# Head-pair attention with a merged window, the residual kept in the output tensor, and sums of FFN2 weights made by DMA

## The chip, the cores and the metric

The kernel runs on one NeuronCore of a Trainium2 chip. The core has five engines with queues of their own: TensorE (PE; its weight loads are shown as PEld), VectorE (DVE), ScalarE (ACT), GpSimd (POOL) and SyncE (SP). SP does no arithmetic here; it issues DMAs, and POOL and ACT issue some too. Each engine works through its instructions in order and waits at semaphores. Arithmetic works on SBUF (128 partitions), PE writes to PSUM, of which each bank holds 128 x 512 float32, and DMAs move data between device memory and SBUF, or within memory. The metric is the device time of one execution in microseconds (us).

## The reference

One decoder layer on 1024 tokens of width 1024, with 16 learned meta tokens put in front (1040 rows in all) and dropped from the output. All in float32:

```python
u = rmsnorm(h, g_pre_mix)
z = u @ w_in                                   # [q 512 | k 128 | v 128 | x 512 | y 512]
attn = sliding_window_attention_with_sinks(q, k, v, sinks)   # 8 heads of 64, 2 KV heads, window 128
rec = gelu(yr) * rg_lru(causal_conv4(xr), ...)               # 512 channels
h = h + rmsnorm(concat(attn, rec) @ w_out, g_post_mix)
u = rmsnorm(h, g_pre_ffn)
f = square(relu(u @ w_ff1)) @ w_ff2            # 1024 -> 4096 -> 1024
out = (h + rmsnorm(f, g_post_ffn))[16:]
```

Attention works in blocks of 128 queries. A query sees the 128 keys up to and with itself, so keys of its own block and of the one before: of each pair of key columns that stand at the same place in the two blocks, exactly one is in the window. The softmax's denominator has one more term, a sink per head. Query heads 0 to 3 use KV head 0, heads 4 to 7 KV head 1.

## The kernel before

**Precision.** A float32 matmul is made of three passes over operands that are split in a high and a low part (`split`, lines 93 to 100: ACT copies with rounding, L95, and DVE subtracts, L98; `mm3`, lines 122 to 128, the passes L124, L125 and L126).

**Order.** The program is written as straight code over tiles in pools; a scheduler makes the order of each engine's queue from it: among the instructions that are ready, it takes the one that stands first in the program, and a DMA into a buffer is ready when the buffer is free. `deferred(1000)` makes some work stand later than written, `behind(name, ins)` pins an order by hand. A tag of the pool `slab` (`raw`, `ws`, `a`, `b`, `c`, `d`, `e`) is a set of buffers that rotate.

**Stages.** (1) Norm, transpose and the projections of K, V, the first pair of Q and the first channels of x, in four pieces of the tokens (`project`, lines 220 to 231). (2) Attention in 4 x 2 rounds (`scores` and `attend`, lines 503 to 594), with the remaining projections as filling for PE (`next_fill`). (3) Gates and recurrence of the LRU. (4) W_out, the norm, and the residual h, which `out_norm` (lines 801 to 823) writes to `h_dram` (L818). (5) FFN1 as seven products of blocks in place of eight (a Strassen scheme: sums of weight blocks and of activation blocks): a first pass with `prep_a`, whose combined weights go to `s_dram` and come back in the second pass (`for p in range(16)`, lines 1066 to 1082, `fetch_b` three tiles ahead), and a third over `third`. (6) FFN2 as seven products too (`PLAN`, lines 1101 to 1110), each in 8 steps over q; a step of `PLAN` names one block of W2 or a sum or difference of two. `fetch_2` (lines 1112 to 1126) loads the terms three steps ahead over SP, or adds the second term by an accumulating DMA from POOL (L1121) for some q; else `prep_2` adds on DVE (L860 through `combine`).

**A round of attention** handles query heads j and j + 4, one of each KV head, and four blocks. Q of a head has its high part on 64 partitions and its low part on the other 64; K's high part is on both halves, its low part on one, with zeros on the other (`put_k`, lines 352 to 357). `scores` makes per head and block a 128 x 256 score tile (own block and the one before), adds the mask and takes the maximum on DVE (L538), the exponential and its sum on ACT (L82), and scales by the reciprocal on DVE (L551). `attend` transposes 128 x 128 pieces on PE (L566), two per block and head, splits them, multiplies with V (`av`, L577), and adds V's high and low results (L591, L592). A round's `attend` stands after the next round's `scores`.

**The end.** Output rows of the second half (four blocks of 128) are finished during FFN2 by `finish_early` (lines 1186 to 1195): scale, a DMA from POOL that adds `h_dram`'s rows in SBUF (L1194), and a store from SP (L1195). Rows of the first half end with the last product: `finish_half` (lines 1199 to 1212) loads h and squares one half of the columns, `finish_late` (lines 1214 to 1244) adds the last product, takes the root on POOL (L169, L1234), multiplies by the gain (POOL, L1237, for three of four), and scales and adds h on DVE (L1241) before two stores. In the last three steps PE goes through row block after row block (lines 1308 to 1312).

Of the kernel before, what the change touches and what calls it, by code (L numbers as in the profile page):

```python
# [9 lines left out]
F32 = mybir.dt.float32  # L10
# [27 lines left out]
def hybrid_layer(  # L38
# [212 lines left out]
    for h in range(2):  # L251
        nc.gpsimd.memset(f32(kl[h][HALF[1 - h]]), 0.0)

    zero = slot("ws", [P, 512])
    nc.vector.memset(zero, 0.0)
    km = const.tile([P, 4, P], F32R, name="km")
    vm = const.tile([P, 2, P], F32R, name="vm")
    nc.vector.tensor_copy(km.rearrange("p a b -> p (a b)"), zero)
    nc.vector.tensor_copy(vm.rearrange("p a b -> p (a b)"), zero[:, :256])
# [65 lines left out]
    rq = fetch([(Q_COL, HD), (Q_COL + 4 * HD, HD)], "e")  # L325
# [26 lines left out]
    def put_k(hh, lo, src):  # L352
        for h in range(2):
            r, o = HALF[h], HALF[1 - h]
            nc.scalar.copy(hh[h][r], src[r])
            nc.vector.tensor_copy(hh[h][o], src[r])
            nc.vector.tensor_tensor(lo[h][r], src[r], f32(hh[h][r]), op=ALU.subtract)  # L357

    def sink_k(acc, t0, n):
        o = 0  # L360
        if t0 == 0:
            m = slice(0, NMETA)
            put_k(
                [km[:, 0, m], km[:, 1, m]], [km[:, 2, m], km[:, 3, m]], acc[:, m]
            )
            o = NMETA
# [4 lines left out]

    def sink_v(acc, t0, n):
        nc.scalar.copy(vt[:, t0 : t0 + n], acc)
# [25 lines left out]
    for b in range(4):  # L399
# [23 lines left out]
        done.append(last_mm[0])  # L423

# [3 lines left out]
    for c in range(NLRU):  # L428
# [18 lines left out]
    nc.gpsimd.memset(mask1[:, 0:P], NEG)  # L447
    nc.gpsimd.memset(mask1[:, 0:NMETA], 0.0)
    nc.gpsimd.affine_select(
        out=mask1[:, 0:NMETA], in_=mask1[:, 0:NMETA], pattern=[[1, NMETA]],  # L450
        compare_op=ALU.is_gt, fill=NEG, base=P - NMETA, channel_multiplier=-1,
    )
    nc.gpsimd.tensor_copy(mask1[:, P:256], mask[:, P:256])
# [32 lines left out]
    nc.tensor.transpose(pv[:NMETA, :P], vt[:, :NMETA], ident)  # L486
    put_v([vm[:NMETA, 0, :], vm[:NMETA, 1, :]], pv[:NMETA, :P])
# [15 lines left out]
    def scores(j, half, q):  # L503
        sn = [slot("c", [P, 4, 257]) for _ in range(2)]
        negm = small.tile([P, 2, 4], F32, name="negm", tag="negm")
        den = small.tile([P, 2, 4], F32, name="den", tag="den")
        rden = small.tile([P, 2, 4], F32, name="rden", tag="rden")
        for h in range(2):
            nc.vector.tensor_copy(
                sn[h][:, :, 256], nsink[:, j + 4 * h : j + 4 * h + 1].to_broadcast([P, 4])  # L510
            )
        for bp in range(2):
            for h in range(2):
# [13 lines left out]
                for i in range(2):  # L527
                    b = 4 * half + 2 * bp + i
                    if b == 0:
                        qk(sp_[:, i, 0:P], b, km[:, h, :], km[:, 2 + h, :])  # L530
                        qk(sp_[:, i, P:256], b, khh[h][:, 0:P], kl[h][:, 0:P])
                    else:
                        c = slice((b - 1) * P, (b + 1) * P)
                        qk(sp_[:, i, :], b, khh[h][:, c], kl[h][:, c])
                for i in range(2):
                    b = 4 * half + 2 * bp + i
                    k = 2 * bp + i
                    nc.vector.tensor_tensor_reduce(  # L538
                        out=sn[h][:, k, 0:256], in0=sp_[:, i, :],
                        in1=mask1 if b == 0 else mask, scale=-1.0,  # L540
                        scalar=nsink[:, j + 4 * h : j + 4 * h + 1],
                        op0=ALU.add, op1=ALU.min, accum_out=negm[:, h, k : k + 1],
                    )
                    lut(
                        sn[h][:, k, :], sn[h][:, k, :], AF.Exp, scale=-1.0,
                        bias=negm[:, h, k : k + 1], accum_out=den[:, h, k : k + 1],
                    )
        for h in range(2):
            nc.vector.reciprocal(rden[:, h, :], den[:, h, :])
            for k in range(4):  # L550
                nc.vector.tensor_scalar(  # L551
# [792 lines left out]
```

## Time and profile before

| | us |
|---|---|
| median of 3 runs | 981.72 (978.06 to 982.81) |
| profiled execution | 980.16 |
| its span, first to last instruction | 978.3 |
| mean granted clock of PE | 0.993 |
| PE busy | 955.2 |
| DVE busy | 680.1 |
| ACT busy | 502.5 |
| POOL busy | 71.3 |
| moved by DMA | 133.28 MB |

Busy time is the union of an engine's instructions. A matmul's recorded length holds its time in the pipeline, so lengths of matmuls overlap and do not add up; what one costs in a stream is read from the distance between starts, which the chain of work that ended last gives. "Idle before, releaser" says how long an engine stood before a group and what it waited for. A name such as `ps_pt<-ident,c` is out <- in by the program's tags.

### The profile page before, as it was taken

The numbers are of one execution on the slowest core, as the hardware profiler recorded it, in microseconds if no ns is written. First come the engines' busy times: TensorE is split into PE (matmuls) and PEld (weight loads), VectorE is DVE, ScalarE is ACT, GpSimd is POOL, SyncE is SP. The second block draws the span as 40 slices with busy tenths as digits, with TensorE's granted clock in tenths as the row PEclk, the third lists the DMA queues.
The fourth block names the chain that finished last, engine by engine and source line by source line (L and its number), as shares of the span: only waits on it lengthen the run. The fifth ranks groups of instructions, "written<-read, shape, count | busy, mean of one in ns | idle before, by whom it ended". The sixth has DMA issues, their size and how long they took to land.

```text
span 978.3 us, 12520 instructions
## 1 busy us (share of the span) xinstructions
PE 955.2 (98%) x4782; PEld 803.4 (82%) x4782; DVE 680.1 (70%) x1002; ACT 502.5 (51%) x809; POOL 71.3 (7%) x108
## 2 busy tenths in 40 slices
PE   7999999999999999999999999999999999999995
PEld 6999998888778878888888888888888888888774
DVE  6669997765975796664644465476668676788685
ACT  7656673558744563443655565564533444344331
POOL 4100000000011100000000000001011000011012
PEclk9999999999999999999999999999999999999988
DMA  8111101112235457686433354334778766658662
GB/s 280 36 38 29 23 28 39 44 44 65 64 130 186 138 172 239 191 258 194 153 106 108 108 175 127 107 102 115 179 185 193 195 215 179 194 156 205 191 173 86
DMA packets 89371, 133.28 MB, mean 136 GB/s; under 512 B 13752, under 2 KB 52680, under 8 KB 89312
## 3 DMA queue, kind: packets, MB, share of 16 engines
q1 hardware_dynamic: 81488, 112.04, 36.4%
q0 software_dynamic: 6960, 18.35, 8.9%
q10 hardware_dynamic: 864, 2.10, 0.6%
q8 instruction: 37, 0.61, 0.3%
q14 instruction: 22, 0.18, 0.1%
HBM read 113.60 MB, written 18.87 MB: 135 GB/s over the span
## 4 chain that ended last, share of the span: by engine, by line
PE 86%; DVE 4%; DMA 3%; issue 2%; ACT 2%; POOL 1%; POOLq 0%; DVEq 0%; SPq 0%; ACTq 0%
PE ps_acc L124 10%; PE ps_acc L125 10%; PE ps_acc L126 10%; PE ps_s L124 6%; PE ps_s L126 6%; PE ps_s L125 6%; PE ps_pt L124 6%; PE ps_pt L126 6%; PE ps_pt L125 6%; PE ps_o L124 5%; PE ps_o L125 5%; PE ps_o L126 5%; DMA raw<-in_w_ff_dram 3%; PE ps_o L577 2%; PE ps_pt L566 1%
## 5 line engine op out<-in xcount | busy, mean ns | idle before, releaser
L95 ACT CAST ws<-raw 128x1024 fp32r<-128x1024 f32 (+1 forms) x70 | 71.7, 1025 | 127.6 <-PE ps_o L125 43.4
L98 DVE TENSOR_TENSOR ws<-raw,ws 128x1024 fp32r<-128x1024 f32 (+1 forms) x71 | 84.7, 1194 | 57.4 <-ACT ws L95 57.4
L124 PE MATMUL ps_acc<-a,ws 128*128 128x256 f32 (+2 forms) x256 | 85.9, 336 | 0.4 <-DVE b L357 0.2
L125 PE MATMUL ps_acc<-a,ws 128*128 128x256 f32 (+2 forms) x256 | 85.5, 334 | 0.0
L126 PE MATMUL ps_acc<-a,ws 128*128 128x256 f32 (+2 forms) x256 | 85.0, 333 | 0.0
L98 DVE TENSOR_TENSOR b<-b,b 128x1024 fp32r<-128x1024 f32 (+2 forms) x48 | 57.6, 1201 | 28.6 <-PE ps_o L125 20.5
L95 ACT CAST ws<-e 128x1024 fp32r<-128x1024 f32 x42 | 43.8, 1044 | 58.7 <-PE ps_o L125 25.9
L95 ACT CAST b<-b 128x1024 fp32r<-128x1024 f32 (+2 forms) x48 | 49.4, 1030 | 40.5 <-DVE b L860 38.5
L98 DVE TENSOR_TENSOR ws<-e,ws 128x1024 fp32r<-128x1024 f32 x42 | 51.4, 1223 | 21.7 <-ACT ws L95 21.6
L124 PEld LDWEIGHTS ps_acc<-a,ws 128*128 128x128 f32 x256 | 48.3, 189 | 4.7 <-DVE b L357 0.5
L126 PEld LDWEIGHTS ps_acc<-a,ws 128*128 128x128 f32 x256 | 48.3, 189 | 4.4
L125 PEld LDWEIGHTS ps_acc<-a,ws 128*128 128x128 f32 x256 | 48.3, 188 | 3.7
L124 PE MATMUL ps_acc<-ws,b 128*128 128x512 f32 (+1 forms) x120 | 46.6, 388 | 2.0 <-ACT ws L95 2.0
L125 PE MATMUL ps_acc<-ws,b 128*128 128x512 f32 (+1 forms) x120 | 46.8, 390 | 0.8 <-DVE ws L98 0.8
L126 PE MATMUL ps_acc<-ws,b 128*128 128x512 f32 (+1 forms) x120 | 46.7, 389 | 0.0
L169 POOL TENSOR_TENSOR rs<-ms,half_pow 128x1 f32<-128x1 f32 (+1 forms) x31 | 20.9, 677 | 346.5 <-DVE ms L165 345.1
L124 PE MATMUL ps_pt<-ws,b 128*128 128x512 f32 x112 | 44.5, 397 | 0.0
L126 PE MATMUL ps_pt<-ws,b 128*128 128x512 f32 x112 | 44.4, 397 | 0.0
L125 PE MATMUL ps_pt<-ws,b 128*128 128x512 f32 x112 | 44.4, 396 | 0.0
L124 PE MATMUL ps_s<-ws,b 128*128 128x512 f32 x110 | 43.9, 399 | 0.0
L125 PE MATMUL ps_s<-ws,b 128*128 128x512 f32 x110 | 43.8, 398 | 0.0
L126 PE MATMUL ps_s<-ws,b 128*128 128x512 f32 x110 | 43.7, 398 | 0.0
(385 smaller groups left out, 2686.8 us busy)
## 6 DMA issues: line engine op xcount, KB each, us to landing
raw<-in_w_ff_dram SPq DMA_DIRECT2D x66, 512.0 KB, 3.8
e<-in_w_ff_dram SPq DMA_DIRECT2D x47, 512.0 KB, 3.7
d<-in_w_ff_dram SPq DMA_DIRECT2D x12, 512.0 KB, 3.8
s_dram<-d POOLq DMA_DIRECT2D x12, 512.0 KB, 3.9
raw<-in_w_in_dram SPq DMA_DIRECT2D x9, 512.0 KB, 4.1
raw<-in_w_ff_dram POOLq DMA_DIRECT2D x9, 512.0 KB, 7.6
c<-in_x_dram SPq DMA_DIRECT2D x8, 512.0 KB, 8.3
d<-in_x_dram SPq DMA_DIRECT2D x8, 512.0 KB, 4.5
```

Source lines behind the costliest of these rows:

```text
L95: nc.scalar.copy(hi, src)
L98: low = nc.vector.tensor_tensor(lo, src, f32(hi), op=ALU.subtract).ins
L124: nc.tensor.matmul(dst, lh, rh, start=start, stop=False, skip_group_check=True)
L125: nc.tensor.matmul(dst, lh, rl, start=False, stop=False, skip_group_check=True)
L126: last_mm[0] = nc.tensor.matmul(dst, ll, rh, start=False, stop=stop, skip_group_check=True).ins.name
L169: last_pow[0] = nc.gpsimd.tensor_tensor(rs[:n], ms[:n], half_pow[:n], op=ALU.pow).ins.name
L566: nc.tensor.transpose(pt[:, o : o + P], sn[h][:, 2 * bp + i, s * P : (s + 1) * P], ident,)
L577: nc.tensor.matmul(po[:, oc : oc + n], v, p_[:, pc : pc + n], start=first and k == 0, stop=last and k == 1, skip_group_check=True,)
```

## The change

**Attention by head pairs.** A round now takes query heads 2j and 2j + 1, which share a KV head. So W_q's columns come in one DMA (`w_q`, `rq`), W_out's rows too (`load_wo`), and K of one KV head needs both parts on both halves of the partitions: `put_k` writes one half, and `mirror_k` copies it to the other by DMA, after the second and the fourth piece of tokens. The meta tokens' K and V stand at the last 16 places of a block before the first. After the softmax the two sides of the window are added into one 128-column tile (POOL) and scaled (DVE), one transpose per block and head follows, and the transposed tile is split back into the two sides by four selects on POOL that write zero outside the triangle. V is multiplied for both heads of the pair at once.

**Residual in the output.** `out_norm` writes h to `out` in place of `h_dram`. The finished rows of the second half and of row blocks 0 and 1 are added to it by an accumulating DMA from POOL into memory. The rows of blocks 2 and 3 still load h; their root is a square root on ACT and a reciprocal on DVE.

**Sums of W2.** For products 2 and 6 the sum of the two weight blocks of each step is made in memory: a copy from SP into `w2_sum` and an accumulating DMA from POOL. The calls stand in the second pass of FFN1; FFN2 loads one tile per step.

```diff
     def w_q(j):
-        return load_cols(
-            [((w_in, Q_COL + HD * j), HD), ((w_in, Q_COL + HD * (j + 4)), HD)]
-        )
+        return load_cols([((w_in, Q_COL + P * j), P)])
...
+    def mirror_k(c):
+        for h in range(2):
+            r, o = HALF[h], HALF[1 - h]
+            for t_ in (khh[h], kl[h]):
+                nc.sync.dma_start(f32(t_[o, c]), f32(t_[r, c]))
...
+        if b == 1:
+            for h in range(2):
+                r, o = HALF[h], HALF[1 - h]
+                nc.sync.dma_start(f32(km[o, h]), f32(km[r, h]))
+            mirror_k(slice(0, 512))
+        elif b == 3:
+            mirror_k(slice(512, T))
...
     def scores(j, half, q):
...
+            nc.vector.reciprocal(rden, den)
+            one = sn[:, :, 0:P]
+            nc.gpsimd.tensor_tensor(one, one, sn[:, :, P:256], op=ALU.add)
+            nc.vector.tensor_tensor(one, one, rden.to_broadcast([P, 4, P]), op=ALU.mult)
+            pairs.append(sn)
+        return pairs
+
+    def attend(j, half, pairs):
+        g = j // 2
+        o_ = slot("e", [P, 512])
+        for bp, sn in enumerate(pairs):
+            mh, ml = pair("c", [P, 4, 2, P])
+            pt = bank("pt", (P, 4, P))
             for k in range(4):
+                nc.tensor.transpose(pt[:, k, :], sn[:, k, 0:P], ident)
+            split(mh[:, :, 1, :], ml[:, :, 1, :], pt)
+            for m in (mh, ml):
+                for side, op, sign in ((0, ALU.is_gt, 1), (1, ALU.is_ge, -1)):
+                    nc.gpsimd.affine_select(
+                        out=m[:, :, side, :], in_=f32(m)[:, :, 1, :],
+                        pattern=[[0, 4], [-sign, P]], compare_op=op, fill=0.0,
+                        base=0, channel_multiplier=sign,
+                    )
+            po = bank("o", (P, 2, 256))
...
+            b = 4 * half + 2 * bp
+            av(vk[g][:, b, :], 0, 256, P, True, False)
+            av(vm[:, g, :] if b == 0 else vk[g][:, b - 1, :], 0, P, 0, False, False)
+            av(vk[g][:, b + 1, :], P, P, 3 * P, False, True)
+            c = slice(256 * bp, 256 * bp + 256)
+            for h in range(2):
+                r, o = HALF[h], HALF[1 - h]
+                nc.scalar.copy(o_[r, c], po[o, h, :])
+                nc.vector.tensor_tensor(o_[r, c], po[r, h, :], o_[r, c], op=ALU.add)
...
-        nc.sync.dma_start(h_dram[t * P : (t + 1) * P, :], h)
+        nc.sync.dma_start(out[t * P : (t + 1) * P, :], h)
...
+    def sum_w2(i, q, terms):
+        for (a, b), kind in zip(terms, ({}, {"accum_op": ALU.add})):
+            (nc.gpsimd if kind else nc.sync).dma_start(w2_sum[i][q], w2v[q, a, b], **kind)
...
     for p in range(16):
+        sum_w2(*((2, p // 2, ((0, 0), (1, 1))), (6, p // 2, ((1, 0), (1, 1))))[p % 2])
         if p + 3 < 16:
             raw_b[p + 3] = fetch_b(p + 3)
...
+        if i in w2_sum:
+            r = slot(tags[0], [P, 2, 512])
+            nc.sync.dma_start(r, w2_sum[i][q])
+            return [r]
...
     def finish_early(j):
...
-        nc.gpsimd.dma_start(o, h_dram[t * P : (t + 1) * P, :], accum_op=ALU.add)
-        nc.sync.dma_start(out[t * P : (t + 1) * P, :], o)
+        nc.gpsimd.dma_start(out[t * P : (t + 1) * P, :], o, accum_op=ALU.add)
...
     def finish_late(j, y, parts):
...
+            if k < len(parts) - 1:
+                combine(o[:, c], acc[:, c], gffn_b[:, c], ALU.mult)
+        if j < 2:
+            nc.scalar.activation(o, o, AF.Copy, scale=rs)
+            nc.gpsimd.dma_start(out[rows, :], o, accum_op=ALU.add)
+            return
+        root = small.tile([P, 1], F32, name="root", tag="root")
+        rs = small.tile([P, 1], F32, name="rs", tag="rs")
+        lut(root, ssq, AF.Sqrt)
+        if j == 2:
             nc.gpsimd.tensor_tensor(o[:, c], acc[:, c], gffn_b[:, c], op=ALU.mult)
         else:
             combine(o[:, c], acc[:, c], gffn_b[:, c], ALU.mult)
+        nc.vector.reciprocal(rs, root)
...
+        if i == 6 and q == 4:
+            root = small.tile([P, 1], F32, name="root", tag="root")
+            lut(root, half_pow, AF.Sqrt, scale=-1.0)
```

More of the change, by code (lines that the diff above doesn't have):

```diff
@@ L250, in hybrid_layer @@
     HALF = (slice(0, HD), slice(HD, P))
[L251 to L256, printed above, removed]
+    km = const.tile([P, 2, 2, P], F32R, name="km")
     vm = const.tile([P, 2, P], F32R, name="vm")
-    nc.vector.tensor_copy(km.rearrange("p a b -> p (a b)"), zero)
-    nc.vector.tensor_copy(vm.rearrange("p a b -> p (a b)"), zero[:, :256])
+    vmt = const.tile([P, P], F32, name="vmt")
+    nc.gpsimd.memset(f32(km), 0.0)
+    nc.gpsimd.memset(vmt, 0.0)
+    META = slice(P - NMETA, P)
     flip = [0]
@@ L446, in hybrid_layer @@
     mask1 = const.tile([P, 256], F32, name="mask1")
[L447 to L453, printed above, removed]
+    nc.gpsimd.memset(mask1[:, 0 : P - NMETA], NEG)
+    nc.gpsimd.tensor_copy(mask1[:, P - NMETA :], mask[:, P - NMETA :])
     lam = prm[:, :, 7]
@@ L485, in hybrid_layer @@
     pv = bank("o")
-    nc.tensor.transpose(pv[:NMETA, :P], vt[:, :NMETA], ident)
-    put_v([vm[:NMETA, 0, :], vm[:NMETA, 1, :]], pv[:NMETA, :P])
+    nc.tensor.transpose(pv[:, :P], vmt, ident)
+    put_v([vm[:, 0, :], vm[:, 1, :]], pv[:, :P])
     for b in range(2):
@@ L555, in scores @@
[L555 to L576 removed]
+                        scalar=nsink[:, 2 * j + h : 2 * j + h + 1],
```

129 lines of the change are left out of this document (44 added, 85 removed).

## The prediction

> **What bounds the kernel now.** I read the page first (busy shares and the chain that ended last), then a table of stages, then what TensorE (PE) waited for.
>
> ```profile
> span 978.3 us, 12520 instructions
> PE 955.2 (98%) x4782; PEld 803.4 (82%) x4782; DVE 680.1 (70%) x1002; ACT 502.5 (51%) x809; POOL 71.3 (7%) x108
> PE 86%; DVE 4%; DMA 3%; issue 2%; ACT 2%; POOL 1%; POOLq 0%; DVEq 0%; SPq 0%; ACTq 0%
> ...
> 36.00:78.00 42.00, 41.65 (x318) 39.50 (x318) 28.75 (x92) 20.52 (x56) 2.71 (x4) 1.00 0.14 32
> 78.00:163.00 85.00, 84.50 (x654) 80.97 (x654) 75.53 (x202) 55.32 (x142) 0.00 (x0) 1.00 0.10 26
> 475.00:575.00 100.00, 100.00 (x434) 81.23 (x433) 50.81 (x57) 55.24 (x57) 0.00 (x0) 1.00 0.38 124
> 900.00:936.00 36.00, 33.26 (x145) 27.04 (x144) 26.16 (x27) 13.94 (x18) 3.39 (x3) 0.92 0.69 199
> 936.00:978.30 42.30, 31.34 (x168) 26.76 (x167) 29.25 (x39) 8.26 (x12) 8.98 (x10) 0.90 0.41 125
> ...
> PE ps_acc L124 <- ACT ws L95: 2.0, 1, 2.0
> PE ps_acc L125 <- DVE ws L98: 0.8, 1, 0.8
> ```
>
> A stage row gives its length, then busy us of PE, weight loads, DVE, ACT and POOL, the granted clock, the DMA share and GB/s. PE is full in the attention stage (84.50 of 85) and in FFN1 (100 of 100). It loses time only in the last stages, where the clock too is below 1. So an edit is worth the matmul time that it takes off PE, plus what it gives back near the end; work taken off another engine elsewhere is worth nothing.
>
> **Attention: less on PE, and new work on POOL.** Per round (one head pair, half the tokens; 8 rounds) the old code makes 16 transposes and 20 attention-value matmuls, the new 8 and 12, since the window's two sides are added before the transpose. Scores keep their 16 matmuls.
>
> ```profile
> 80.28 0.44 PE ps_pt L566 x4
> 89.76 0.98 PE ps_o L577 x9
> 99.55 0.53 PE ps_o L577 x5
> 937.25 0.23 PE ps_pt L124
> 938.06 0.12 PE ps_o L125
> ...
> L566 PE MATMUL ps_pt<-ident,c 128*128 128x128 f32 x128 | 19.3, 275 | 0.0
> L577 PE MATMUL ps_o<-c,b 128*128 128x256 f32 x96 | 18.4, 297 | 0.0
> L577 PE MATMUL ps_o<-c,b 128*128 128x128 f32 x48 | 9.1, 247 | 0.5 <-DVE c L98 0.4
> L577 PE MATMUL ps_o<-c,vm 128*128 128x128 f32 x16 | 3.4, 232 | 0.0
> ```
>
> The first five rows are steps of the chain, so they give what a matmul costs in the stream and not its pipelined length: 0.11 us a transpose (0.44/4), 0.23 us a 512-column matmul, 0.12 us a 256-column one; ten value matmuls of a head are about 0.98 x 10/9 = 1.05 us (0.53 for five agrees). The group rows give the counts. Transposes: 64 fewer x 0.11 = 7.0 us. Values: 16 heads x 1.05 = 16.8 us become 8 x (4 x 0.23 + 8 x 0.12) = 15.0 us, a gain of 1.8. Together -8.8 us, all on the path.
>
> DVE loses eight 256-wide multiplies and two subtractions a round and gains two 512-wide multiplies and two short additions: lighter, and off the path, so nothing is counted. POOL, idle in this stage, gets per round two additions of 128x512 and eight selects that write 128x512.
>
> ```profile
> L1237 POOL TENSOR_TENSOR a<-a,a 128x512 f32<-128x512 f32 x3 | 4.0, 1337 | 15.3 <-ACT a L1183 15.3
> L437 POOL MEMSET mask<- 128x256 f32 x1 | 0.3, 301 | 0.0
> L438 POOL TENSOR_SCALAR_AFFINE_SELECT mask<-mask 128x128 f32<-128x128 f32 x1 | 0.3, 292 | 0.1
> 75.00:165.00 90.00, 17.60 (x80) 1.00 0.10 26
> ```
>
> An addition is 1.34 us. The trace has selects of 128 columns only (0.29). Four times that is 1.17; if only a memset's slope scales (about 0.8 ns a column from its row), 0.29 + 384 x 0.8 ns = 0.6. I take 0.85, between them. A round costs POOL 2 x 1.34 + 8 x 0.85 = 9.5 us (7.5 to 12.0). (The Trainium skill, GPSIMD Engine Reference, "Performance versus the Vector engine", gives 1.03 to 1.8 cycles of 1.2 GHz an element for simple bodies; an estimate from it is 0.44 to 0.77 us a select, cheaper than the rows make it, and the sum by it would leave out the 3 us taken below and end at 963. No run here has that width yet.) The last row is the score reductions (L538, two records each, eight a round): 5 rounds in 90 us, 18 us a round. So POOL has room, but the selects stand in the latency between the transposes of two blocks and their value matmuls: 4 x 0.85 = 3.4 us (2.4 to 4.7) in each of 16 places where the old code had nothing. PE's order is fixed and projections fill it; if the order leaves room for the selects, the price is 0, if none of it is hidden 16 x 4.7 = 75 us. I take 3 us, near the hidden end of 0, because DVE and ACT already stand in the same place in the old code and PE still got 84.50 of 85 us.
>
> **K mirror, loads.** Ten 64-partition DMAs now copy K into the other half (before: DVE casts), and wait on SP for the K sinks; queued behind them are the next weight loads. W_q and half of W_out come in one DMA instead of two (eight fewer). PE's cover is 36:78, where projections of later tokens keep it full. Counted 0; if a mirror is late the scores stand for one landing, at most the slowest kind below (7.6 us). A gain at the start of up to 1 us is left out.
>
> **FFN2's end: the starved stretch.**
>
> ```profile
> SPq L1195 <- DMA a<-h_dram: 22.1, 4, 8.0
> ...
> 920.04 8.41 DMA raw<-in_w_ff_dram
> 928.55 1.05 ACT ws L95
> 930.91 0.79 PE ps_acc L125
> 936.82 0.43 PE ps_pt L126
> ```
>
> SP waited 22.1 us to store rows whose residual an accumulating DMA was adding; the W2 loads stood behind it in SP's queue, and on the chain one load took 8.41 us. PE then waited 2.0 + 0.8 us (quoted above) and ran at 0.43 us a matmul instead of 0.23 from 930.91 until 937.25. That stretch of 6.3 us holds one step of 0.79 and 13 of 0.43; at 0.23 the 14 are 3.2 us, so 3.1 us were lost to the clock. The change takes the store off SP (the accumulating DMA writes the output itself), and the last product loads one ready sum a step, not two terms; POOL's nine accumulating loads (six and three, by the conditions on q) and DVE's seven additions in products 2 and 6 go too. Late next is the single load of a step, asked for three steps (3 x 24 matmuls x 0.23 = 17 us) ahead: hidden, even at the 8.41 us above. -2.8 - 3.1 = -5.9 us. Bounds: 0 to -6.
>
> **The tail.**
>
> ```profile
> 967.06 0.28 PE L126 MATMUL ps_acc<-a,b 128*128 128x256 f32 x1
> 967.89 2.77 DVE L1241 SCALAR_TENSOR_TENSOR a<-a,rs,d 128x512 f32<-128x512 f32 x3
> 971.65 0.41 DVE L860 TENSOR_TENSOR a<-ps_acc,a 128x256 f32<-128x256 f32 x1
> 972.09 0.48 DVE L1227 CUSTOM_DVE_ANT_0 a<-a,part 128x256 f32<-128x256 f32 x1
> 973.75 1.41 DVE L1241 SCALAR_TENSOR_TENSOR a<-a,rs,d 128x512 f32<-128x512 f32 x2 [0.44 <-POOL rs L1234]
> ```
>
> PE ends at 967.3; the addition that needs it starts only at 971.65, behind final writes of earlier rows on DVE. The span ends at 978.3, 11 us after PE and 3.1 after the last DVE instruction. Now rows 0 and 1 finish on ACT and an accumulating DMA, and the last root is on ACT and DVE instead of POOL. After PE remain 0.41 + 0.48 + some 0.5 (root, reciprocal, hand-overs) + 1.41 + 3.1 = 5.9 us if DVE is free, so up to -5. Against it: row block 1's chain of seven steps and a landing of 7.6 us (row below) may end last, little before. I take -4; bounds 0 and -5. A table load for the root falls two steps earlier, under ACT's 8.26 of 42.30.
>
> **W2's sums in memory.** 16 copies (SP) and 16 accumulates (POOL), 0.5 MB each, added.
>
> ```profile
> q1 hardware_dynamic: 81488, 112.04, 36.4%
> q0 software_dynamic: 6960, 18.35, 8.9%
> raw<-in_w_ff_dram POOLq DMA_DIRECT2D x9, 512.0 KB, 7.6
> 557.88 0.50 SPq L1202 DMA_DIRECT2D d<-h_dram  x1
> ```
>
> Per MB, q1 holds all 16 engines for 0.364 x 978/112 = 3.2 us, q0 4.7 us: a copy 1.7 us (double if reading and writing memory add up), an accumulate 2.5: 67 to 94 us for all. But where? The last row is the residual load that the code asks for in FFN2's last product, in the last 60 us, and it was issued at 557.88, long ahead of its place, when its buffer came free: a DMA that waits for nothing is issued as soon as its queue is free. The copies need no buffer. So I expect them not in FFN1's second pass but in the first 100 us, where DMA's share is 0.14 and 0.10 and 67 to 94 us have room. Cost 0. Without that cover: in the second pass (16 tiles x 24 matmuls x 0.23 = 88 us, 0.38 of it taken) 55 us are free for 67 to 94; loads run up to 39 us late, less the three tiles of lead (17 us): up to 22 us.
>
> **Sum.** The profiled execution took 980.2 (span 978.3 and 1.9 around it), 1.6 below the median, 981.7. -8.8 + 3 - 5.9 - 4 = -15.7: 964.5 from that execution, 966 from the median; I say 965.
>
> **Rivals.** *A: attention becomes bound by POOL (slower).* For it:
>
> ```profile
> 962.46 1.29 POOL L1237 TENSOR_TENSOR a<-a,a 128x512 f32<-128x512 f32 x1 [15.29 <-ACT a L1183]
> 962.70 1.07 DVE L165 SCALAR_TENSOR_TENSOR ms<-sq,late 128x1 f32<-128x1 f32 x1
> 964.29 0.14 DVE L165 SCALAR_TENSOR_TENSOR ms<-sq,late 128x1 f32<-128x1 f32 x1
> ```
>
> The same one-column DVE instruction took 1.07 us beside POOL's addition and ended with it, and 0.14 alone. DVE is 75.5 of 85 us busy in attention; ten POOL instructions a round could each hold one up, or be held. If PE then stands 2 us at each of the 16 places: 32 us, 981.7 - 18.7 + 32 = 995. It ends slower once PE stands more than (18.7 + 4.9)/16 = 1.5 us a place. Against it: POOL's 9.5 us in a round of 18. Chance 0.11. The Trainium skill, SBUF — State Buffer, "Who interferes with whom", states the mechanism: a DVE instruction with two SBUF inputs and a GpSimd one that reads SBUF exclude each other for the whole instruction; the two L165 rows agree. By that rule the DVE and POOL times add where both read SBUF, and the sum would lean to this rival.
>
> *B: the sums collide.* In the second pass (as written) up to 22 us: 966 + 22 = 988; half of that, 977, is likelier, since the accumulates may lag until product 2 reads the sums. At the start the price is the same wait, before x's or W_in's loads. For it: the copies stand ahead of the mirrors and W_in loads in SP's queue, and POOL must wait for each copy before the next root of the input norms. Against it: 0.86 of DMA's time is free from 36 on. Chance 0.09.
>
> *C: the end stays starved or the tail is not shortened* (the new accumulating stores end last): 966 + 5.9 + 4 = 976. Chance 0.12, faster still. *D: gains and stalls cancel by pieces*: within 0.5%, 0.05. My forecast, 959 to 971: 0.63.
>
> **Chances.** 0.5% is 4.9 us, about what this kernel's runs can tell from none. Faster: the forecast 0.63, C 0.12 and 0.04 of B = 0.79. Same: D 0.05, 0.02 of B and 0.02 of A = 0.09. Slower: 0.09 of A and 0.03 of B = 0.12. The low end, 956, is every term at its better bound (8.8 + 6 + 5 + 1 from 980.2 is 959) and run-to-run spread; the high end, 982, takes in C, half of B and D, and leaves most of A out.
>
> **What would show it.** Right: 64 transposes and 96 value matmuls; PE still full in attention; POOL near 76 us there; no PE wait and no clock below 1 before PE's end; the span ending 7 us after PE; copies of W2 issued in the first 100 us. Wrong: PE waits on POOL behind the selects, a select above 1.2 us, PE waiting for s_dram or W_in loads, or for the K mirror.

## The result, and the profile after

The changed kernel takes 1057.0 us (median of four runs, 1055.5 to 1058.8) against 981.8 for the kernel before in the same comparison: a ratio of 1.079, 95% interval 1.076 to 1.082. It is slower by 75 us, where 965 us and a gain were forecast. The profiled execution took 1055.5, its span 1053.8.

The page of the changed kernel: busy times, the share of engines in the chain that ended last, and PE's busy tenths and granted clock in 40 slices of 26 us.

```profile
span 1053.8 us, 12315 instructions
PE 956.5 (91%) x4654; PEld 800.8 (76%) x4654; DVE 654.9 (62%) x935; ACT 499.5 (47%) x816; POOL 150.1 (14%) x191
PE   7247159989999899999999999999999999999997
PEclk9758669999999999999999999999999999999999
PE 74%; issue 8%; DVE 6%; DMA 4%; ACT 4%; POOL 2%; SPq 2%; DVEq 0%; POOLq 0%; ACTq 0%
```

Nearly all of the loss lies in the first six slices. The table of stages says the same (columns as in the prediction: length, busy us of PE, weight loads, DVE, ACT and POOL, granted clock, DMA share, GB/s); the last three rows answer to FFN1 and to the two last stages of the kernel before.

```profile
0.00:36.00 36.00, 26.27 (x189) 24.93 (x189) 18.29 (x38) 23.26 (x48) 12.33 (x28) 1.00 0.98 308
36.00:78.00 42.00, 10.44 (x48) 9.74 (x49) 6.59 (x15) 5.28 (x13) 6.25 (x10) 0.57 0.81 204
78.00:163.00 85.00, 44.20 (x298) 41.49 (x297) 23.84 (x72) 16.76 (x47) 14.08 (x15) 0.75 0.48 81
560.00:660.00 100.00, 100.00 (x434) 81.36 (x433) 50.86 (x57) 55.72 (x57) 0.05 (x1) 1.00 0.39 124
975.50:1011.50 36.00, 36.00 (x163) 29.53 (x162) 30.46 (x31) 16.27 (x21) 2.68 (x3) 1.00 0.47 119
1011.50:1053.80 42.30, 35.67 (x196) 30.67 (x194) 25.10 (x40) 12.22 (x19) 10.88 (x7) 0.98 0.30 74
```

Between 36 and 78 us PE is busy for 10.4 us, where it was for 41.7. The late stages have the look that was forecast: PE full in the last but one, at clock 1.00, and 35.67 us busy in the last, at 0.98. So the time splits at one place that both kernels pass, the transposes after W_out. The answers for that line, of the kernel before and then of the changed kernel (lengths in ns, then first and last start):

```profile
L834 PE MATMUL ps_o<-ident,d x64: 269/273/273, 296.7 to 347.9; 128*128 128x128 f32 x64
```
```profile
L835 PE MATMUL ps_o<-ident,d x64: 269/273/273, 383.0 to 434.3; 128*128 128x128 f32 x64
```

And PE's last matmul in the timeline of the changed kernel (start, length):

```profile
1046.89 0.28 PE L126 MATMUL ps_acc<-a,b 128*128 128x256 f32 x1
```

Up to the transposes the changed kernel lost 383.0 - 296.7 = 86.3 us. From there to PE's last matmul it takes 663.9 us against 670.4 (6.5 less), and from that to the end 6.9 against 11.2 (4.3 less). 86.3 - 6.5 - 4.3 = 75.5.

What PE waited for in the changed kernel, and then POOL (engine, line <- releaser: us in total, times, longest):

```profile
PE ps_acc L124 <- DVE b L351: 34.6, 2, 33.6
PE ps_s L286 <- DVE d L213: 28.7, 2, 22.9
PE ps_s L286 <- DVE a L117: 10.1, 1, 10.1
PE ps_o L286 <- DVE d L213: 8.1, 2, 7.0
```
```profile
POOL w_sum L889 <- issue: 85.4, 14, 10.2
```

Its timelines of POOL and then DVE (start, length, what, and in brackets the idle time before and who ended it):

```profile
53.73 1.05 POOL L889 DMA_DIRECT2D w_sum<-in_w_ff_dram  x1 [9.36 <-DMA w_sum<-in_w_ff_dram]
...
55.17 0.57 POOL L169 TENSOR_TENSOR rs<-ms,half_pow 128x1 f32<-128x1 f32 x1
62.54 1.11 POOL L889 DMA_DIRECT2D w_sum<-in_w_ff_dram  x1 [6.81 <-issue]
...
69.94 1.15 POOL L889 DMA_DIRECT2D w_sum<-in_w_ff_dram  x1 [6.00 <-issue]
70.56 1.15 POOL L169 TENSOR_TENSOR rs<-ms,half_pow 128x1 f32<-128x1 f32 x1
...
138.07 1.53 POOL L467 TENSOR_TENSOR sm<-base_e,sm 128x4 f32<-128x4 f32 x1
```
```profile
55.77 0.75 DVE L213 TENSOR_SCALAR d<-c,rs 128x1024 f32<-128x1024 f32 x1 [24.52 <-POOL rs L169]
...
139.63 0.17 DVE L468 TENSOR_SCALAR sm<-sm 128x4 f32<-128x4 f32 x1 [35.73 <-POOL sm L467]
```

Read it from the bottom. DVE stood 24.5 us for the root of a norm and 35.7 us for a power of four numbers (L467), both on POOL. POOL had issued the accumulates of W2 between them, one every 6 to 12 us, and stood between most of them for nothing that the profile shows ("issue"). DVE works in order, so K's low parts (L351) and the normed x (L213) stood behind, and PE with them: 81.5 us in the four rows. After each stop PE ran at half clock for a while (0.57 and 0.75 in the stages), which together with the waits makes up the loss; the two were not separated further. The last of these small POOL instructions gives the size of the loss by itself: L467 starts at 138.07 us, and in the kernel before (there L462) at

```profile
55.08 1.02 POOL L462 TENSOR_TENSOR sm<-base_e,sm 128x4 f32<-128x4 f32 x1 [14.59 <-DVE sm L461]
```

that is 83.0 us earlier.

### The profile page after: what moved, and what is told of

It reads as the page before. It is cut to its first block, busy times and chain, and to the rows that moved or that the text cites. A ratio compares the mean times of both kernels' runs of the same rounds, so it can differ in the third digit from the quotient of the medians.

```text
span 1053.8 us, 12315 instructions
## 1 busy us (share of the span) xinstructions
PE 956.5 (91%) x4654; PEld 800.8 (76%) x4654; DVE 654.9 (62%) x935; ACT 499.5 (47%) x816; POOL 150.1 (14%) x191
## 4 chain that ended last, share of the span: by engine, by line
PE 74%; issue 8%; DVE 6%; DMA 4%; ACT 4%; POOL 2%; SPq 2%; DVEq 0%; POOLq 0%; ACTq 0%
PE ps_acc L124 8%; PE ps_acc L125 8%; PE ps_acc L126 8%; PE ps_pt L126 6%; PE ps_pt L125 6%; PE ps_pt L124 6%; PE ps_s L126 6%; PE ps_s L125 6%; PE ps_s L124 6%; PE ps_o L125 5%; PE ps_o L124 5%; PE ps_o L126 5%; DMA w_sum<-in_w_ff_dram 3%; DVE c L545 1%; POOL w_sum L889 1%
## 5 line engine op out<-in xcount | busy, mean ns | idle before, releaser
L95 ACT CAST ws<-raw 128x1024 fp32r<-128x1024 f32 (+1 forms) x70 | 71.7, 1024 | 127.3 <-PE ps_o L125 47.9
L124 PE MATMUL ps_acc<-a,ws 128*128 128x256 f32 (+2 forms) x256 | 89.7, 350 | 34.8 <-DVE b L351 34.6
L125 PE MATMUL ps_acc<-a,ws 128*128 128x256 f32 (+2 forms) x256 | 88.6, 346 | 0.0
L126 PE MATMUL ps_acc<-a,ws 128*128 128x256 f32 (+2 forms) x256 | 88.4, 346 | 0.0
L124 PEld LDWEIGHTS ps_acc<-a,ws 128*128 128x128 f32 x256 | 52.3, 204 | 40.2 <-issue 33.8
L169 POOL TENSOR_TENSOR rs<-ms,half_pow 128x1 f32<-128x1 f32 (+1 forms) x31 | 23.4, 758 | 258.1 <-DVE ms L165 256.7
L125 PEld LDWEIGHTS ps_acc<-a,ws 128*128 128x128 f32 x256 | 52.2, 204 | 4.1
L126 PEld LDWEIGHTS ps_acc<-a,ws 128*128 128x128 f32 x256 | 52.0, 203 | 4.4
L575 POOL TENSOR_SCALAR_AFFINE_SELECT c<-c 128x512 fp32r<-128x512 f32 x64 | 47.2, 755 | 23.2 <-ACT c L95 10.2
L124 PE MATMUL ps_acc<-ws,b 128*128 128x512 f32 (+1 forms) x120 | 46.1, 384 | 0.0
L124 PE MATMUL ps_pt<-ws,b 128*128 128x512 f32 x112 | 44.0, 393 | 0.0
L124 PE MATMUL ps_s<-ws,b 128*128 128x512 f32 x110 | 43.4, 395 | 0.0
L126 PE MATMUL ps_s<-ws,b 128*128 128x512 f32 x110 | 43.3, 394 | 0.0
```

Source lines behind the costliest of these rows:

```text
L95: nc.scalar.copy(hi, src)
L124: nc.tensor.matmul(dst, lh, rh, start=start, stop=False, skip_group_check=True)
L125: nc.tensor.matmul(dst, lh, rl, start=False, stop=False, skip_group_check=True)
L126: last_mm[0] = nc.tensor.matmul(dst, ll, rh, start=False, stop=stop, skip_group_check=True).ins.name
L169: last_pow[0] = nc.gpsimd.tensor_tensor(rs[:n], ms[:n], half_pow[:n], op=ALU.pow).ins.name
L575: nc.gpsimd.affine_select(out=m[:, :, side, :], in_=f32(m)[:, :, 1, :], pattern=[[0, 4], [-sign, P]], compare_op=op, fill=0.0, base=0, cha ...
```

## The experiments

Ratios are to the kernel before, run beside each experiment on the same chip, with 95% intervals. That kernel's own runs lay between 973.5 and 983.8 us over all comparisons, so single times are read only where tens of us are in question. Its median depends on the chip, too: 974.5 us beside e1, e2, e3 and e5, 979.8 beside e6, e7 and e9. So where some us matter, stretches of the traces are compared. The theory of the traces is called P: POOL's queue, not the traffic, the attention or the mirrors, holds PE at the start. Its rivals A, M and D, and S and L for the missing gain of the attention, are named in the expectations.

### The sums alone, left out, and behind the roots

**Without the sums** (product 2 and 6 load two terms as before):

```diff
-        sum_w2(*((2, p // 2, ((0, 0), (1, 1))), (6, p // 2, ((1, 0), (1, 1))))[p % 2])
```

> The changed kernel without the W2 sums (products 2 and 6 load their two terms as before); attention by head pairs and the residual in the output stay. Theory P (the loss is POOL's queue: 16 accumulates ahead of the roots of the input norms): all of the loss goes, and what is left is the gain of the other parts, 964 to 972 us. Theory A (attention is bound by POOL's selects and additions): it stays above 985. Theory M (the K mirror's DMAs hold PE): the stalls before the first scores stay, above 1000.

975.7 us, ratio 1.000 (0.998 to 1.002). The whole loss is gone with the sums. That excludes the mirrors and a POOL-bound attention as causes of it. But the other parts gain nothing together, which none of the theories said; "Where the other gains went" takes that up.

**The sums alone**, added to the kernel before:

```diff
+        sum_w2(*((2, p // 2, ((0, 0), (1, 1))), (6, p // 2, ((1, 0), (1, 1))))[p % 2])
...
+        if i in w2_sum:
+            r = slot(tags[0], [P, 2, 512])
+            nc.sync.dma_start(r, w2_sum[i][q])
+            return [r]
```

> The kernel before with the W2 sums alone. Theory P: the same roots stand behind the same accumulates, so about the same 75 to 90 us are lost, less up to 6 us at FFN2's end: 1050 to 1070 us, with PE standing for tiles of x that wait for POOL's root. Theory A or M (another part of the change is needed for the loss): below 1000.

1056.8 us. Nothing else of the change is needed for the loss. Its accumulates come at the same times (24.6 to 137.5 us), and PE's longest wait, 36.4 us, is the same one (`PE ps_acc L124 <- DVE b L357`).

**The same, accumulates behind the roots:**

```diff
+    last_early = nc.gpsimd.tensor_tensor(ee, base_e, nabs, op=ALU.pow).ins.name
...
+            if kind:
+                behind(last_early, ins)
```

> The kernel before with the W2 sums alone, all copies where they were in SP's queue, and the 16 accumulates placed in POOL's queue behind the last small POOL instruction of the start (the power of the LRU's constants). The DMAs are the same and still lie in the first 200 us. Theory P: 975 to 995 us, since no root stands behind an accumulate. Rival D (the 67 to 94 us of DMA traffic at the start are what delays the loads): the loss stays, above 1030.

972.3 us (one run; the runs of the kernel before beside it: 973.5 to 980.8). Its timeline of POOL, and the answer for the scores of the meta tokens' keys, the first of all:

```profile
55.21 1.02 POOL L462 TENSOR_TENSOR sm<-base_e,sm 128x4 f32<-128x4 f32 x1 [14.49 <-DVE sm L461]
56.19 1.29 POOL L888 DMA_DIRECT2D w_sum<-in_w_ff_dram  x1
63.25 1.07 POOL L888 DMA_DIRECT2D w_sum<-in_w_ff_dram  x1 [5.77 <-issue]
...
160.51 1.06 POOL L888 DMA_DIRECT2D w_sum<-in_w_ff_dram  x1 [5.27 <-issue]
```
```profile
L518 PE MATMUL ps_s<-km,b x8: 220/222/305, 60.7 to 173.5; 128*128 128x128 f32 x8
```

The copies stand where they stood in SP's queue, the accumulates still come 7.0 us apart (16 from 56.2 to 160.5), and the first scores come at 60.7 us as in the kernel before. The traffic at the start costs nothing that can be seen; the place in POOL's queue costs 84 us (1056.8 - 972.3).

**Why 6.6 us each?** In the program an accumulate waits for its own copy only, and from the ninth on for the accumulate eight places before it; the "issue" gaps are neither. To see whether it is room for descriptors, the memory of POOL's DMA queue was doubled in the kernel with the sums alone (to make room, small tiles rotate over three buffers in place of four, and constants share a tile):

```diff
-        "TRN2", target_bir_lowering=False, num_devices=1, dynamic_dma_scratch_size=1024
+        "TRN2", target_bir_lowering=False, num_devices=1, dynamic_dma_scratch_size=2048
```

> The kernel before with the W2 sums alone, as in e2 (accumulates ahead of the roots), with the memory for the descriptors of POOL's DMA queue doubled from 1024 to 2048 bytes a partition (small tiles rotate over three buffers in place of four to make room). If POOL stands because that memory has room for about one accumulate: the accumulates come some 3 us apart in place of 6.6 and the loss of 82 us falls by a third or more, to 1000 to 1030 us. If the accumulating transfers themselves take 6.6 us each, one after the other: still 6.4 to 6.9 us apart and 1045 to 1058 us.

1006.9 us. The accumulates come closer, in POOL's timeline of this kernel:

```profile
74.19 1.05 POOL L889 DMA_DIRECT2D w_sum<-in_w_ff_dram  x1 [5.89 <-issue]
78.19 1.04 POOL L889 DMA_DIRECT2D w_sum<-in_w_ff_dram  x1 [2.95 <-issue]
82.04 1.03 POOL L889 DMA_DIRECT2D w_sum<-in_w_ff_dram  x1 [2.81 <-issue]
...
87.94 1.05 POOL L889 DMA_DIRECT2D w_sum<-in_w_ff_dram  x1 [1.93 <-issue]
88.53 1.52 POOL L463 TENSOR_TENSOR sm_all<-sm_all 128x4 f32<-128x4 f32 x1
```

From 63 to 88 us they are 3.5 us apart on average (1.5 to 6.9), the small power is at 88.5 us where it was at 138.1 in e2, and 50 of the 82 us come back. So POOL stands for room in that memory, not for a transfer that can only run alone. The Trainium skill (DMA: Bandwidth & Descriptors, "SWDGE vs HWDGE vs iDMA") says that GpSimd computes the descriptors of its DMAs itself and appends them to rings in a carve-out of SBUF; this run agrees, and adds that POOL's later instructions stand while the ring has no room. How many accumulates fit was not measured.

### Other places for the sums

**Both in FFN1's second pass**, as the code reads, each copy held behind the load of `s_dram` ahead of it:

```diff
+            if not kind:
+                behind(fetched[0], ins)      # the last load of s_dram
```

> The changed kernel with each copy placed in SP's queue behind the load of the second pass of FFN1 that the code has ahead of it, so that copies and accumulates do run in that pass. Theory P: no root waits, and the pass has room: 960 to 970 us, the start as without the sums. Rival B as predicted (the sums collide with the second pass's loads): 977 to 988, with PE waiting for s_dram's loads between 575 and 700 us.

974.8 us, ratio 0.998 (0.995 to 1.000), between the two ranges expected. The loss is gone, the pass has nearly room: its DMA share rises from 0.37 to 0.90 between 475 and 575 us, and PE waits 2.3 us for `t_dram`'s loads at its end (578 us). So rival B's 22 us, priced for this pass, is 2.3 us and the clock behind it. The accumulates come 6.5 to 10.8 us apart here.

**Copies at the start, accumulates in FFN1's first pass:**

```diff
+            if kind:
+                behind(stored[2 * q + i // 4], ins)      # POOL's stores to s_dram
```

> The changed kernel with its copies left at the start and each accumulate placed in POOL's queue behind a store of the first pass of FFN1. Theory P: no root waits, and the copies alone (8.4 MB read and written before 60 us) delay nothing that PE needs: 968 to 975 us, first scores near 60 us as without the sums. If the copies' traffic delays x, W_in or the mirror by itself: first scores after 70 us and above 985.

986.9 us, ratio 1.010 (1.007 to 1.013): a miss. The first scores come at 60.5 us as hoped, but between 352 and 475 us the DMA share is 0.91 and PE is busy for 112.3 of 123 us. The stage's row and the waits of DVE and SP in it, of this kernel:

```profile
352.00:475.00 123.00, 112.32 (x462) 87.61 (x461) 73.84 (x101) 49.61 (x77) 21.81 (x27) 0.97 0.91 244
```
```profile
DVE d L861 <- DMA d<-in_w_ff_dram: 20.4, 6, 6.5
```
```profile
SPq L858 <- DMA s_dram<-d: 25.9, 6, 7.6
```

SP's weight loads wait longer for POOL's stores to leave their buffers (25.9 us in this stretch, 19.1 without sums), and DVE for the weights (20.4 us, 9.9 without sums). There the accumulates and the loads of FFN1 share a stretch that has no room for both.

**Copies behind the weight loads of FFN1's third pass** (with the early root pinned, below):

```diff
+        fetched[0] = w1_load(r1, 1, p, 0, 2).ins.name      # in fetch_c
...
+            if not kind:
+                behind(fetched[0], ins)
```

> The whole change, with the root in its place as in e12 and each W2 copy placed in SP's queue behind a weight load of FFN1's third pass (accumulates follow on POOL by their own copies). If the parts add: the attention's 0.6%, a tail some 4 us shorter and no stall at 578 us as in the second pass, 966 to 971 us, a ratio of 0.988 to 0.993. If the sums' traffic delays weight loads there: PE waits for raw or ws between 690 and 780 us, a ratio of 0.995 to 1.000.

976.8 us, ratio 0.999 (0.997 to 1.002): PE waits for ws there, as the second case said (3.4 and 0.8 us from 694 us on, with the clock behind it), and 1.8 us for `t_dram`.

### Where the other gains went

**The attention alone** and **the residual with the tail alone**, each added to the kernel before. The first takes the change's edits of `w_q` to `attend` and `load_wo`, the second these:

```diff
-        nc.sync.dma_start(h_dram[t * P : (t + 1) * P, :], h)
+        nc.sync.dma_start(out[t * P : (t + 1) * P, :], h)
...
     def finish_early(j):
     def finish_half(j):
     def finish_late(j, y, parts):
```

> The kernel before with the head-pair attention alone (with the K mirror and the new order of the weights' columns). Theory S: the 8.8 us that PE is spared are given back as stalls between 88 and 265 us: 974 to 979 us against 974.5. By the prediction: 5.8 less, 968 to 970.

> The kernel before with the residual kept in the output and the new tail alone. By the prediction's terms (5.9 at FFN2's end, 4 in the tail) 10 us less than a run of the kernel before in which the end starves, so 968 to 972. If the starved end is not in most runs of the kernel before, only the tail is left: 970 to 974 against 974.5. If accumulating stores end last: no gain, 974 to 977.

Attention: 973.6 us, ratio 0.9939 (0.9924 to 0.9954). Residual and tail: 976.0 us, ratio 0.9964 (0.9939 to 0.9989). Both expectations give times against 974.5, the median of the kernel before on another chip; here it was 979.8.

The attention's ratio is what the prediction's terms give (-5.8 us of 980), but that gain does not lie in the attention. The stage from 78 to 163 us and the transposes after W_out, with the attention alone (e9):

```profile
78.00:163.00 85.00, 79.20 (x554) 73.22 (x553) 70.40 (x169) 50.05 (x139) 49.96 (x54) 0.98 0.09 26
```
```profile
L836 PE MATMUL ps_o<-ident,d x64: 270/272/273, 297.3 to 348.7; 128*128 128x128 f32 x64
```

PE stands for 5.8 of the 85 us, where it stood for 0.5, and the transposes start at 297.3 us, no earlier than in the kernel before (296.7). The same cut for the other runs, at the starts of the first scores, of these transposes and of PE's last matmul (us, one execution each):

| | to the first scores | to W_out's transposes | to PE's last matmul | to the end |
|---|---|---|---|---|
| before | 60.6 | 236.1 | 670.4 | 11.2 |
| before, again (e8) | 60.4 | 236.2 | 666.4 | 11.1 |
| attention alone (e9) | 60.1 | 237.2 | 663.5 | 11.0 |
| residual and tail alone (e7) | 62.7 | 237.2 | 665.1 | 10.3 |
| the change without sums (e1) | 59.3 | 240.3 | 664.9 | 9.6 |
| e1 without the selects (e6) | 59.2 | 232.8 | 663.6 | 9.9 |
| e1 with the root held back (e12) | 59.4 | 236.6 | 663.7 | 10.1 |
| sums alone, behind the roots (e5) | 60.7 | 236.4 | 664.2 | 9.1 |
| residual, tail, sums, root held back (e14) | 60.7 | 236.2 | 664.5 | 7.0 |
| the change | 108.7 | 274.3 | 663.9 | 6.9 |

In its own stretch, the second, the attention alone gains nothing: PE is busy for 229.1 us in place of 234.9 and stands for 8.1 in place of 1.2, as theory S said. By the traces its shorter time comes from the third stretch, where it has no edit of FFN1 or FFN2: there the kernel before met late loads in both profiled executions, and e9 did not. Whether the attention makes late loads rarer, or its four runs happened to have none, is not shown.

**Without the selects** (from the kernel without the sums; the value matmuls read one unselected tile, so the window's triangles are left out of the output):

```diff
-            mh, ml = pair("c", [P, 4, 2, P])
+            mh, ml = pair("c", [P, 4, P])
...
-            split(mh[:, :, 1, :], ml[:, :, 1, :], pt)
-            for m in (mh, ml):
-                for side, op, sign in ((0, ALU.is_gt, 1), (1, ALU.is_ge, -1)):
-                    nc.gpsimd.affine_select(
...
+            split(mh, ml, pt)
```

> The changed kernel without the W2 sums and without the 64 selects: both sides of the window are multiplied with the same unselected tile, so the triangle is left out of the result; PE's instructions and POOL's additions stay. Theory S (POOL's selects stand between transposes and value matmuls and give back the gain of the head-pair attention): PE's stalls of some 10 us between 88 and 217 us go, 963 to 968 us against 975.7 with the selects. Rival L (the LRU's chain on DVE and ACT, for which PE waited at 261.5 us, sets that time anyway): the stall at 261 grows by what the attention gains, and the time falls by less than 3.

968.9 us, ratio 0.9893 (0.9876 to 0.9910) against 1.000 with them. The stage from 78 to 163 us, first with the selects (e1), then without:

```profile
78.00:163.00 85.00, 79.17 (x553) 73.16 (x552) 70.29 (x166) 49.70 (x139) 50.00 (x54) 0.98 0.09 26
```
```profile
78.00:163.00 85.00, 83.42 (x584) 77.35 (x583) 71.43 (x173) 51.57 (x140) 14.32 (x10) 1.00 0.11 32
```

PE loses 5.8 us with them and 1.6 without, and the clock dips with them. Theory S holds: from the first scores to W_out's transposes the kernel takes 240.3 us with the selects and 232.8 without, so they give back 7.5 us. PE's waits in e1 name the selects for 2.5 us of it; the rest was not split further. L falls: the stop at the LRU's end is 2.7 us, no longer than with the selects (2.6).

**The early root.** At that stop, with the sums left out (e1), ACT's timeline shows a table load for the root that the code asks for in FFN2's last product, and PE's timeline the wait behind it:

```profile
261.58 1.28 ACT L82 ACT_TABLE_LOAD   x1
262.87 0.20 ACT L82 ACTIVATE root<-half_pow 128x1 f32<-128x1 f32 x1
262.98 1.03 ACT L95 CAST a<-d 128x1024 fp32r<-128x1024 f32 x1
```
```profile
264.58 0.50 PE L124 MATMUL ps_pt<-a,b 128*128 128x512 f32 x1 [2.64 <-ACT b L95]
```

It waits for a constant only, and so was placed some 660 us early (e12 has it at 925.2 us), into the chain for which PE waits. (The Trainium skill, ScalarE: Activation LUTs, "What ACT_TABLE_LOAD costs", gives some 1283 ns for the load; the rows' 1.28 us agree.) Held back:

```diff
             lut(root, half_pow, AF.Sqrt, scale=-1.0)
+            behind(high[0], last_lut_ins[0])      # the last split's copy on ACT
```

> The changed kernel without the W2 sums, with the early root (the square root of a constant that brings ACT's table in ahead of the last rows) placed in ACT's queue behind the split of FFN2's last product. If the table load at 256 us is what PE's stall of 3.0 us at 261.5 and the half clock behind it come from: the stall falls to about 1 us, as with the attention alone, and the time by 2 to 4 us, to a ratio of 0.996 to 0.998 where it was 1.0001. If it is not: the stall stays and the ratio is 1.000 again.

973.4 us, ratio 0.9953 (0.9932 to 0.9974), and PE's wait there is 1.1 us. Two instructions of together 1.5 us cost 3.7 us (240.3 and 236.6 in the table), by the stop and the half clock behind it (in e1 PE's matmuls start 0.43 us apart until 268.3 us, then 0.23), and some 1 us with the old attention (237.2 in e7, which has the root at 262.3 us, and 236.2 in e14). Without the selects and without this root the stretch would be some 229.1 us (an estimate, 232.8 - 3.7): 7.0 less than in the kernel before, and the selects take 7.5. So no gain is missing in e1: the attention comes to about 0, and the root on top of it.

**The kernel before, again**, with no edit:

> The kernel before, profiled again on this chip, where most of its runs take 974 us and some 980. If the 6 us between them are the starved end: a profile near 974 shows PE full and the clock at 1.00 from 900 to 936 us and no wait on ws there, and one near 980 shows the waits of the first profile. If the end starves in both, the 6 us lie elsewhere.

976.1 us. A late stage's row and PE's longest wait behind the start:

```profile
900.00:936.00 36.00, 36.00 (x175) 30.00 (x174) 31.62 (x33) 15.22 (x19) 4.67 (x4) 1.00 0.81 214
```
```profile
PE ps_acc L125 <- DVE ws L98: 1.9, 1, 1.9
```

The starved end is not in this execution, and the third stretch of the table is 666.4 us for 670.4; it has one late weight instead, at 774.5 us, for which PE waits 1.9 us. So which load comes late differs from one execution to the next, and the first profile showed a bad one.

### Versions that beat both

The residual and the tail (e7) with the sums behind the roots of the start (e5), the old attention:

```diff
+            if kind:
+                behind(last_early, ins)
...
-        nc.gpsimd.dma_start(o, h_dram[t * P : (t + 1) * P, :], accum_op=ALU.add)
-        nc.sync.dma_start(out[t * P : (t + 1) * P, :], o)
+        nc.gpsimd.dma_start(out[t * P : (t + 1) * P, :], o, accum_op=ALU.add)
```

> The kernel before with the residual and the tail of the change and with the W2 sums, whose accumulates stand behind the last small POOL instruction of the start; the old attention. If the three gains add (the tail some 4 us shorter, no starved end, 16 loads and 7 DVE additions fewer in FFN2): 966 to 970 us, 0.5 to 1.2% under the kernel before on the same chip. If the end was bound by PE anyway: within 0.3% of it.

972.0 us, ratio 0.9943 (0.9924 to 0.9962). With the early root held back as in e12:

> The kernel before with the residual, the tail and the W2 sums, accumulates behind the roots of the start as in e10, and the early root in its place. If the early table load cost e10 its 1 us at 265 us: a ratio of 0.992 to 0.9945 against 0.9943, no more.

970.6 us, 0.9926 (0.9902 to 0.9950). And with the attention too, sums for product 6 only, accumulates behind the last select:

```diff
+    w2_sum = {i: dpool.tile([8, P, 2, 512], F32, name=f"w2_sum{i}") for i in (6,)}
...
+            if kind:
+                behind(last_select[0], ins)
```

> The change with the sums of product 6 alone (product 2 loads its terms as before), the copies at the start, the 8 accumulates placed in POOL's queue behind the attention's last select, and the early root in its place. Theory P: 8 x 6.6 = 53 us of accumulates from about 207 us on, ended at 260 before the roots of the output norms come at some 290, so they delay nothing, and the tail is the short one (7 us behind PE's end where e12 had 9.8): a ratio of 0.990 to 0.994. If something waits for POOL's queue there too, or the 4 MB of copies at the start delay loads: 0.995 or more.

970.2 us, ratio 0.9917 (0.9890 to 0.9943). The eight accumulates start from 204.9 to 255.5 us, 6.4 to 8.3 us apart, and the next root follows at 280.1. Nothing waits for them. e14 and e15 can't be told apart.

## Why the prediction was wrong, step by step

**The failed step** is "W2's sums in memory ... Cost 0". It had the place right: the copies were issued from 14 to 48 us, the accumulates from 23.5 to 137.5, not in the second pass. It had the traffic right: e5 carries it at the start for nothing. It judged the cover by DMA's share alone. The scarce thing was POOL's queue, in which 16 accumulates of 6.6 us stood ahead of roots on which PE's first matmuls depend. Rival B had this sentence ("POOL must wait for each copy before the next root of the input norms") but priced it as one late transfer, up to 22 us, since no row of the profile before showed accumulates back to back; the runs show 84. Its mechanism was the smaller part, too: POOL stood 11.0 us for copies (in two waits) and 85.4 in the gaps that e11 puts down to room for descriptors.

**Attention: the work about right, the stalls too small.** It had -8.8 on PE and "I take 3 us" of stalls, -5.8 together. The -8.8 is about 7.0 by e6 and e12; the selects' stalls are 7.5 us, 0.47 at each of the 16 places, and the stretch of the attention alone comes out 1.1 us longer. That its ratio of 0.9939 equals the -5.8 is luck. The argument for 3 us was that DVE and ACT already stood in the same place and PE still got 84.50 of 85 us; with POOL there as well it gets 79.20. Rival A named this cost, and would have needed 1.5 us at each place to end slower. PE's busy time fell from 955.2 to 946.7 us (e1; in the changed kernel the half clock lengthens it again). The price of one instruction was not the error: the selects took 0.76 us for an estimate of 0.85, the additions 1.52 for 1.34 (groups of the changed kernel):

```profile
L575 POOL TENSOR_SCALAR_AFFINE_SELECT c<-c 128x512 fp32r<-128x512 f32 x64 | 47.2, 755 | 23.2 <-ACT c L95 10.2 <-DVE c L98 9.5 <-DVE c L516 2.3
L559 POOL TENSOR_TENSOR c<-c 128x512 f32<-128x512 f32 x16 | 24.3, 1518 | 53.8 <-ACT c L82 53.7
```

**Mirrors: right at 0.** With the attention alone the first scores come at 60.1 us, before at 60.6.

**FFN2's end:** -5.9 was forecast, and the stretch from W_out's transposes to PE's end is 6.5 shorter in the changed kernel. That agreement is luck too: with the attention alone, which changes nothing there, it is 6.9 shorter. The starved stretch belonged to one execution (e8 has none), so the term was sized on a sample of one. Over several runs the residual with the tail gives 0.36%, 3.5 us (1.1 to 6.0), where 9.9 stood in the sum.

**Tail:** -4 forecast; from PE's last instruction's end to the span's end it is 10.9 us before and 6.6 after. The new order of the tail, which the prediction named, is the smaller part: with the new tail alone it is 10.0 (e7), with the sums alone and the old tail 8.8 (e5), with both 6.7 (e10, e14). In e7 DVE's timeline shows no pause from 963.98 us to its end, and one instruction that takes 1.99 us:

```profile
963.98 1.99 DVE L1227 CUSTOM_DVE_ANT_0 a<-a,late 128x256 f32<-128x256 f32 x1
```

The same instruction takes 0.47 us in e14. With the sums alone DVE starts the addition that needs PE's last matmul 2.2 us after PE's end (963.80 us in e5) where it took 4.3 before. That DVE has fewer additions left with one load a step fits this, but was not tried apart.

**The early root:** "falls two steps earlier, under ACT's 8.26 of 42.30" is wrong by some 660 us, and what was put at nothing costs 3.7 us (e1 and e12), although the rule that placed it is the one quoted for the copies: what waits for nothing is issued at once.

## What to carry to other kernels

An instruction that waits for nothing is placed as early as its queue allows, whatever line it stands on; list everything new that has no inputs from the kernel (DMAs between tensors in memory, a table load for a constant), and see what stands behind each in its engine's queue. A queue is a resource of its own: a DMA issued from an engine that also computes can hold that engine for the length of the transfer, and idle DMA engines say nothing about it. One profiled execution shows that something can happen, not how often; a term taken from a single stall needs a second execution. And a time that agrees with a term does not show the term: cut the traces at places that both kernels pass, and see in which stretch the gain lies.

## What the runs showed of the hardware

Accumulating DMAs of 0.5 MB from memory to memory, issued one after the other from POOL, came 7.0 us apart on average with 1024 bytes a partition for their descriptors (e5) and 3.5 with 2048 (e11, from 63 to 88 us); the issue itself takes 1.05 us of POOL's time, the rest is standing. PE at half clock is seen at its first transposes after a stop of 22.9 us: 0.21 us apart where they were 0.11 before it (PE's timeline of the changed kernel).

```profile
33.33 0.27 PE L286 MATMUL ps_o<-ident,d 128*128 128x128 f32 x1
33.44 0.27 PE L286 MATMUL ps_s<-ident,d 128*128 128x128 f32 x1
...
56.58 0.48 PE L286 MATMUL ps_s<-ident,d 128*128 128x128 f32 x1 [22.87 <-DVE d L213]
56.85 0.42 PE L286 MATMUL ps_pt<-ident,d 128*128 128x128 f32 x1
57.06 0.42 PE L286 MATMUL ps_o<-ident,d 128*128 128x128 f32 x1
```
